# Whole float32 products for the first layer's input projections, and attention's PSUM as three more accumulators

## The chip, the cores and the metric

The kernel runs on one core of one Trainium2 chip. The metric is device time in microseconds (us) of one execution, the median of the runs shown. Five engines take part: TensorE (PE in the profile, with its weight loads as PEld), VectorE (DVE), ScalarE (ACT), GpSimd (POOL) and SyncE (SP), which here only issues the loads of the weights. Each engine works through its own queue in order; semaphores tie the queues together.

## The reference

One step of a two-layer trunk, for 256 prompt positions and 8 sample rows, all float32:

```
for l in range(2):
    h = rmsnorm(x, attn_norm_g[l])
    q, k, v, u = split(h @ w_in[l])        # 2048 -> 1024 + 128 + 128 + 1024
    a = sliding-window attention(rope(q), rope(k), v, sinks)   # 16 heads, window 128
    s = S5 state space over u (64 groups of 16 channels, 64 states each), then z * sigmoid(z @ w_glu + b)
    x = x + concat(rmsnorm(a), rmsnorm(s)) @ w_out[l]
    up = rmsnorm(x) @ w_up[l]              # 2048 -> 2 * 5632
    x = x + (silu(conv(g)) * conv(val)) @ w_down[l]
y = rmsnorm(x)
```

The last rows of k and v, the final states and the last up-projected rows are returned as well.

## The kernel before

The activations are kept transposed: 128 features on the partitions and 264 columns (256 prompt positions and 8 sample rows), so the model width of 2048 is 16 tiles `x[0]` to `x[15]` of 128x264. A *product* gives one tile of 128 output features: it runs over the chunks `k` of the contraction (16 for a projection in, 8 for `oa`, `glu` and `os`), and adds them up in one PSUM accumulator.

**One chunk is three matmuls.** A float32 weight chunk `w` is split as `w = wh + wl`, and the activation as `h = hh + hl`, each part in the type float32r, and `product` issues `wh*hh`, `wh*hl` and `wl*hh`. The weights come from HBM as tiles `raw` of 8 chunks (512 KB, four buffers, loaded in order by SP). `Stream.prep_to` makes from each half of a `raw` tile (a *unit*, 4 chunks, 128x512) the tile `wh`, a cast on ACT (sometimes on DVE), and `wl = raw - wh`, a subtraction on DVE (on POOL for the first four units and where the planner finds DVE late). `Stream.get` is called at each fourth chunk, prepares 4 or 5 units ahead of the one used, and asks for the `raw` tile three ahead. The first layer's activations `h` are split before the layers begin, one ACT and one DVE instruction for each of the 16 tiles; other activations go through `split`.

**Order of the work.** The program is written out by a planner (`Plan`, `Engine.cost`) that keeps a modelled time for each engine. `ORDERS[l]` fixes the order of a layer's products. Between any two chunks `side.tick()` lets the waiting side tasks (generators: attention heads, SSM steps, evictions, norms) issue instructions whose inputs are ready by the modelled times; PE's queue, like the others, is then worked through in that order. `side.until(cond)` ticks, and moves the modelled PE time on, until the condition holds.

**A layer.** `mix_phase` runs 18 projections in (`k`, `v`, `q0` to `q7`, `u0` to `u7`), then 13 or 14 products `oa` (attention's part of the projection out), `glu0` to `glu7`, the rest of `oa`, and `os0` to `os15` (the SSM's part). While the projections run, side tasks rotate q and k, do the eight pairs of attention heads (`heads`), one sample task, and the SSM of each `u` tile in two halves (`ssm_pair`: matmul `xps`, then on DVE `m`, `xr`, four scans, `n`, `G`; then matmul `yps`). The task `ssm_prep` makes the SSM's tables on POOL. A `z` tile (the input of `glu`) needs the SSM of its `u` tile; all eight are needed for each `glu`. Then `ffn_phase` streams the up and down projections, 44 + 44 products of 16 chunks and 48 of 16, 16 and 12.

**Accumulators.** `s_acc` holds two PSUM accumulators for all products. `acc_tile` waits (by modelled time) until one is free; the task that evicts the accumulator gives it back (`take_u`, `take_v`, `take_kq`, `add_half`, `gate_task`, `conv`, `down`). `take_u`, `take_v` and `add_half` need the factor of an RMSNorm (`norm_h.rb`, `norm_a.rb`, `norm_s.rb`) first. Attention has three more PSUM tiles of its own in a mix phase, `s_sps` (two) and `s_ops` (one). The products `os0` and `os1` take their accumulators from `s_sps`; nothing else does after attention.

Of the kernel before, what the change touches and what calls it, by code (L numbers as in the profile page):

```python
# [10 lines left out]
F32 = mybir.dt.float32  # L11
# [28 lines left out]
          "oa11 oa12 glu0 oa13 glu1 glu2 glu3 glu4 glu5 glu6 glu7 oa14 oa15 os0 os1 os2 os3 os4 os5 os6 os7 os8 "  # L40
          "os9 os10 os11 os12 os13 os14 os15").split())
NUNITS = DEPTH * 2720 // UNIT


class Engine:
# [264 lines left out]
def tile_hymba_step(ctx: ExitStack, tc: tile.TileContext, w, xT, consts, gains, small, kc, vc, vc0, ssm_bc, ssm_h0, convp, sconv, kraw, vraw, craw,  # L310
# [14 lines left out]
    s_acc = Slots(nc, ps_acc, "acc", 2, [P, NT])  # L325
    s_ev = Slots(nc, np_, "ev", 2, [P, NT])

    def acc_tile(name):
        side.until(s_acc.there)
        return s_acc.tile(name)  # L330

    bank = Sem(nc, 1)

# [4 lines left out]
    class Stream:  # L338
# [17 lines left out]
        def prep_to(self, n):  # L356
            while self.prep < min(n, NUNITS):
                i = self.prep
                self.load_to(i // 2 + 1)
                src = self.raw[i // 2][:, (i % 2) * UNIT * P:(i % 2 + 1) * UNIT * P]  # L360
                wh = wp.tile([P, UNIT * P], F32R, tag="wh", name=f"wh{i}", bufs=5)
                if i >= 8 and nc.t["dve"] < nc.t["pe"] + -500.0 and nc.t["act"] > nc.t["pe"] + 1000.0:
                    nc.vector.tensor_copy(wh, src)
                else:
                    nc.scalar.copy(wh, src)
                self.wh[i] = (wh, src)
                if i % 2:
                    del self.raw[i // 2]
                self.prep += 1
            while self.low < min(n - (n > 8), NUNITS):  # L370
                i = self.low
                wh, src = self.wh.pop(i)
                wl = wp.tile([P, UNIT * P], F32R, tag="wl", name=f"wl{i}", bufs=4)
                (nc.gpsimd if i < 4 or (nc.t["pool"] < nc.t["pe"] + 0.0 and nc.t["dve"] > nc.t["pe"] + 2000.0) else nc.vector).tensor_tensor(wl, src, wh.bitcast(F32), ALU.subtract)
                self.ready[i] = (wh, wl)
                self.low += 1
# [11 lines left out]
    def product(acc, n, chunk):  # L388

        for k in range(n):  # L390
            if k % UNIT == 0:
                wh, wl = ws.get()
            side.until(lambda: chunk(k) is not None)
            j = (k % UNIT) * P
            hl = chunk(k)
            nc.tensor.matmul(acc, wh[:, j:j + P], hl[:, 0, :], start=(k == 0), stop=False)
            nc.tensor.matmul(acc, wh[:, j:j + P], hl[:, 1, :], start=False, stop=False)
            nc.tensor.matmul(acc, wl[:, j:j + P], hl[:, 0, :], start=False, stop=(k == n - 1))
            side.tick()
# [7 lines left out]

    def set_tiles(s, i, name):
        return setp.tile([P, 2, NT], F32R, tag=f"set{s}_{i}", name=name)


    x = []
# [357 lines left out]
    def mix_phase(l, sets, h, norm_h):  # L770
# [160 lines left out]
        AT = [None] * 8  # L931
        norm_a = Norm(f"a{l}", 1024)
        s_raw, s_rot = Slots(nc, mp, "qraw", 3, [P, NT]), Slots(nc, mp, "qrot", 2, [P, NT])
        s_sps, s_ops = Slots(nc, pm, "sps", 2, [P, 3, P]), Slots(nc, pm, "ops", 1, [P, NPR])
        s_sm, s_mx, s_pT = Slots(nc, mp, "sm", 2, [P, 2, 3 * P]), Slots(nc, mp, "mx", 2, [P, 4, 2, 2]), Slots(nc, mp, "pT", 2, [P, 3, P])

        def rotate(raw, dst, nm):
# [46 lines left out]
        def heads(i, qrot):  # L984
# [47 lines left out]
                    nc.vector.tensor_copy(pT[hh], pps)  # L1032
                    s_sps.give("dve", pps)
            s_sm.give("pe", sm)
            ops = opsd[i] = yield from s_ops.take(f"ops{l}{i}")
            yield "pe", *pT
            for cols, blk, j, first, final in ((slice(0, P), 0, 0, True, True), (slice(P, NPR), 0, 1, True, False),
                                               (slice(P, NPR), 1, 2, False, True)):
# [126 lines left out]
        def take_u(m, acc):  # L1165
            yield from norm_h.wait()
            ude = Y[m]
            rb = norm_h.rb
            yield "dve", acc, rb
            nc.vector.tensor_tensor(ude[:, 0:NPR].rearrange("p (j c) -> p j c", j=2),  # L1170
                                    acc[:, 0:NPR].rearrange("p (c j) -> p j c", j=2),
                                    rb[:, 0:NPR].rearrange("p (c j) -> p j c", j=2), ALU.mult)
            nc.vector.tensor_tensor(ude[:, NPR:], acc[:, NPR:], rb[:, NPR:], ALU.mult)
            s_acc.give("dve", acc)
            side.add(ssm(m, ude), 1)

        def take_v(acc):
            yield from norm_h.wait()
            vsb = yield from s_raw.take(f"vsb{l}")
            yield "dve", acc, norm_h.rb  # L1180
            nc.vector.tensor_tensor(vsb, acc, norm_h.rb, ALU.mult)
            s_acc.give("dve", acc)
            side.add(v_task(vsb))

        def take_kq(nme, acc):
            raw = yield from s_raw.take(f"raw{l}{nme}")
            yield "act", acc
            nc.scalar.copy(raw, acc)
            s_acc.give("act", acc)
            side.add(k_task(raw) if nme == "k" else q_task(int(nme[1]), raw))  # L1190
            if nme == "q7":
                side.add(sample_task(), 0)
# [1 line left out]

        halves = set()

        def add_half(m, acc, norm, nm, own=False, eng="pool"):
            yield from norm.wait()
            t = yield from s_ev.take("ev" + nm)
            yield "dve", acc, norm.rb  # L1200
            nc.vector.tensor_tensor(t, acc, norm.rb, ALU.mult)
            if not own:
                s_acc.give("dve", acc)
            if eng == "pool":
                yield "pool", t
            (nc.gpsimd if eng == "pool" else nc.vector).tensor_tensor(x[m], x[m], t, ALU.add)
            s_ev.give(eng, t)
            halves.add(nm)
# [6 lines left out]
        def gate_task(m, acc):  # L1215
            s2 = yield from s_s2.take(f"s2{l}{m}")
            th = yield from s_ev.take(f"th{l}{m}")
            yield "act", acc
            nc.scalar.activation(th, acc, AF.Tanh, bias=hvec[:, l * 16 + 8 + m:l * 16 + 9 + m], scale=0.5)
            s_acc.give("act", acc)  # L1220
            if m == 7:
                warm()
            yield "dve", th
            nc.vector.scalar_tensor_tensor(s2[:, 0:NPR].rearrange("p (c j) -> p j c", j=2),
                                           th[:, 0:NPR].rearrange("p (j c) -> p j c", j=2), 1.0,
                                           Y[m][:, 0:NPR].rearrange("p (j c) -> p j c", j=2), ALU.add, ALU.mult)
            nc.vector.scalar_tensor_tensor(s2[:, NPR:], th[:, NPR:], 1.0, Y[m][:, NPR:], ALU.add, ALU.mult)
            s_ev.give("dve", th)
            stt = set_tiles(sB, m, f"s{l}{m}")
            yield from split(stt, s2, hgs[:, l * 8 + m:l * 8 + m + 1])  # L1230
            norm_s.add(s2, last=m == 7)
            s_s2.give("act", s2)
            S[m] = stt
            if m == 7:
                norm_s.start()
# [5 lines left out]
        def residual(m, acc):  # L1241
            while f"a{l}{m}" not in halves:
                yield None
            yield from add_half(m, acc, norm_s, f"s{l}{m}", m < 2, "pool" if m < 14 else "dve")
            hl = set_tiles(sC if m < 8 else sA, m % 8, f"h2{l}{m}")
            yield from split(hl, x[m], gain(l, 3, m))
            norm_f.add(x[m])
            h2[m] = hl
            if m == DK - 1:
                norm_f.start()  # L1250
# [2 lines left out]
        lastin = [n for n in ORDERS[l] if n[0] in "uqkv"][-1]  # L1253
        for nme in ORDERS[l]:
            kind, m = nme.rstrip("0123456789"), int(nme.lstrip("uqkvoasgl") or 0)
            if kind == "os" and m < 2:
                side.until(s_sps.there)
                acc = s_sps.tile(f"os{l}{m}", [P, NT])
            else:
                acc = acc_tile((f"in{l}{nme}" if kind in "uqkv" else f"{kind}{l}{m}"))  # L1260
            if kind == "oa":
                product(acc, 8, lambda k: AT[k] if f"A{k}" in done else None)
                side.add(add_half(m, acc, norm_a, f"a{l}{m}"), 0)
# [6 lines left out]
            else:  # L1270
                product(acc, DK, lambda k: h[k])
                side.add(take_u(m, acc) if kind == "u" else take_v(acc) if kind == "v" else take_kq(nme, acc), -2)
                if nme == lastin:
                    done.add("in")
        side.until(lambda: norm_s.rb is not None and "attn" in done)
        mctx.close()
        return h2, norm_f

    def ffn_phase(l, sets, h2, norm_f):
# [20 lines left out]
        def conv(acc, f, rf):  # L1300

            e = s_E.pop()
            nc.vector.tensor_tensor(e[:, 2:], acc, rf, ALU.mult)
            s_acc.give("dve", acc)
            c = s_cv.tile(f"cv{l}{f}")
            return c, conv_gen(c, e, f)

# [61 lines left out]
        def down(m, acc, last):  # L1369
            yield "dve", acc  # L1370
            nc.vector.tensor_tensor(x[m], acc, x[m], ALU.add)
            s_acc.give("dve", acc)
            if last:
                yield "act", x[m]
                norm_n.add(x[m], last=m == DK - 1 and l == DEPTH - 1)
# [49 lines left out]
    for k in range(DK):  # L1425
        if k % UNIT == 1:
            for j in ((0, 1), (2,), (3,), ())[k // UNIT]:
                norm_h.add(x[j], eng=nc.gpsimd)
            ws.prep_to(k // UNIT + 1)
        hl = set_tiles(sets[0] if k < 8 else sets[1], k % 8, f"h{k}")  # L1430
        nc.scalar.activation(hl[:, 0, :], x[k], AF.Copy, scale=gain(0, 0, k))
        some_params(1)
        nc.vector.scalar_tensor_tensor(hl[:, 1, :], x[k], gain(0, 0, k), hl[:, 0, :].bitcast(F32), ALU.mult, ALU.subtract)
        h[k] = hl

    def squares():
        for k in range(4, DK):
# [171 lines left out]
```

## Time and profile before

| | |
|---|---|
| median of 3 runs | 2337.96 us (2332.14 to 2338.8) |
| profiled execution: its time | 2339.3 us |
| profiled execution: its span | 2337.5 us |
| TensorE clock granted, mean over the span | 0.973 of full speed |
| PE busy | 2208.3 us (94%) |
| DVE busy | 1718.0 us (73%) |
| ACT busy | 1272.4 us (54%) |
| POOL busy | 673.7 us (29%) |

All times in the profile count from the start of the span. The busy time of PE includes the pipelined end of each matmul, so it is an upper bound of the time in which the array takes columns. The trace gives most instructions the line of a helper (L116), so they are told apart by the names of their tiles: `in0q<-h,wh` is a matmul of a `q` projection of layer 0, `wl<-raw,wh` the subtraction, `xps`, `m`, `xr`, `n`, `G`, `yps` the steps of the SSM, `sps`, `sm`, `pps`, `ops` those of attention, `eva` and `evs` the evictions of `oa` and `os`.

### The profile page before, as it was taken

To read this page: it belongs to the slowest core of one execution; us is meant where nothing else is said; L and a number is where in the kernel's file an instruction comes from. 1 tells how busy PE (TensorE), PEld (TensorE's weight loads), DVE (VectorE), ACT (ScalarE), POOL (GpSimd) and SP (SyncE) were. 2 spreads that over 40 slices of the span, in tenths; PEclk is the share of its full clock that TensorE was granted. 3 is DMA by queue.
4 is the path that set the end of the run, shared out by engine and by line. 5 is a ranking of instruction groups with operands and counts; after the bars stand their busy time and mean duration, and the time that the engine had idled before them with its cause. 6 is when DMAs were issued, how large, how long until landed. Compare 5 with 4: busy or idle time off the path is not lost.

```text
span 2337.5 us, 47944 instructions
## 1 busy us (share of the span) xinstructions
PE 2208.3 (94%) x18300; PEld 2145.2 (92%) x18300; DVE 1718.0 (73%) x3227; ACT 1272.4 (54%) x2493; POOL 673.7 (29%) x895
## 2 busy tenths in 40 slices
PE   7988799999999999999998878999999999999997
PEld 6866688999999999999997767989999999999997
DVE  8898987877657776577778979777775677756764
ACT  5655455555445554455555564655554455545554
POOL 6565636711001110011236555341110011101112
PEclk9999899999999999999999989999999999999998
DMA  6322344555655555555553313545555555555553
GB/s 201 128 74 81 102 139 163 174 181 181 198 181 179 180 192 185 180 179 191 190 166 105 106 65 117 170 163 179 180 180 182 179 181 181 181 181 181 180 188 128
DMA packets 107447, 378.24 MB, mean 162 GB/s; under 512 B 14386, under 2 KB 16706, under 8 KB 107168
## 3 DMA queue, kind: packets, MB, share of 16 engines
q1 hardware_dynamic: 101664, 361.10, 46.3%
q0 software_dynamic: 3248, 13.48, 1.9%
q8 instruction: 144, 2.36, 0.4%
q10 hardware_dynamic: 2304, 0.59, 0.1%
q14 instruction: 87, 0.71, 0.1%
HBM read 371.18 MB, written 6.73 MB: 162 GB/s over the span
## 4 chain that ended last, share of the span: by engine, by line
PE 73%; DVE 6%; POOL 2%; issue 1%; ACT 0%; DMA 0%; DVEq 0%; ACTq 0%; POOLq 0%
PE d L116 22%; PE g L116 21%; PE v L116 21%; PE oa L116 2%; PE in1q L116 1%; DVE wl L116 1%; DVE xr L116 1%; PE glu L116 1%; PE os L116 1%; PE in1u L116 1%; DVE m L116 1%; DVE G L116 1%; POOL ssq_f L116 1%; POOL x L116 0%; DVE sm L116 0%
## 5 line engine op out<-in xcount | busy, mean ns | idle before, releaser
L116 DVE TENSOR_TENSOR wl<-raw,wh 128x512 fp32r<-128x512 f32 x1323 | 978.3, 743 | 368.7 <-PE d L116 171.1
L116 ACT CAST wh<-raw 128x512 fp32r<-128x512 f32 x1358 | 836.3, 620 | 712.8 <-PE d L116 236.8
L116 PE MATMUL g<-h,wh 128*128 128x264 f32 x2816 | 524.2, 286 | 1.7 <-DVE E L116 1.1
L116 PE MATMUL v<-h,wh 128*128 128x264 f32 x2816 | 521.7, 285 | 0.0
L116 PE MATMUL d<-ff,wh 128*128 128x264 f32 x2816 | 516.0, 284 | 0.0
L116 PEld LDWEIGHTS g<-h,wh 128*128 128x128 f32 x2816 | 441.1, 190 | 2.5 <-DVE E L116 1.5
L116 PEld LDWEIGHTS v<-h,wh 128*128 128x128 f32 x2816 | 439.2, 189 | 0.2
L116 PEld LDWEIGHTS d<-ff,wh 128*128 128x128 f32 x2816 | 436.9, 188 | 0.0
L116 POOL COPY cout<-E 128x10 f32<-128x10 f32 x176 | 100.6, 572 | 1148.1 <-DVE E L116 1148.1
L116 PE MATMUL g<-h,wl 128*128 128x264 f32 x1408 | 404.3, 287 | 0.0
L116 PE MATMUL v<-h,wl 128*128 128x264 f32 x1408 | 402.8, 286 | 0.0
L116 PE MATMUL d<-ff,wl 128*128 128x264 f32 x1408 | 400.5, 284 | 0.0
L116 PEld LDWEIGHTS g<-h,wl 128*128 128x128 f32 x1408 | 266.9, 190 | 0.0
L116 PEld LDWEIGHTS v<-h,wl 128*128 128x128 f32 x1408 | 265.5, 189 | 0.0
L116 PEld LDWEIGHTS d<-ff,wl 128*128 128x128 f32 x1408 | 265.1, 188 | 0.0
L116 DVE SCALAR_TENSOR_TENSOR cv<-E,cw,cv 128x256 f32<-128x256 f32 x352 | 174.4, 496 | 21.5 <-ACT cv L116 2.4
L116 PE MATMUL oa<-a,wh 128*128 128x264 f32 x512 | 109.4, 311 | 28.6 <-DVE eva L116 18.4
L116 PEld LDWEIGHTS oa<-a,wh 128*128 128x128 f32 x512 | 88.0, 208 | 33.7 <-issue 20.3
L116 ACT ACTIVATE cv<-E,cw 128x264 f32<-128x264 f32 x176 | 106.9, 609 | 2.3 <-DVE E L116 2.3
L116 PE MATMUL os<-s,wh 128*128 128x264 f32 x512 | 95.7, 286 | 3.7 <-DVE evs L116 3.5
L116 PEld LDWEIGHTS os<-s,wh 128*128 128x128 f32 x512 | 79.4, 188 | 6.4 <-issue 4.2
L116 DVE TENSOR_TENSOR E<-g,rb_f 128x264 f32<-128x264 f32 x88 | 38.0, 432 | 59.2 <-PE g L116 59.2
(316 smaller groups left out, 3026.7 us busy)
## 6 DMA issues: line engine op xcount, KB each, us to landing
raw<-in_w_dram SPq DMA_DIRECT2D x680, 512.0 KB, 3.3
bc<-in_ssm_bc_dram POOLq DMA_DIRECT2D x16, 256.0 KB, 3.2
x<-in_xT_dram SPq DMA_DIRECT2D x16, 132.0 KB, 3.9
out_dram<-hn SPq DMA_DIRECT2D x8, 264.0 KB, 2.6
sc<-in_sconv_dram POOLq DMA_DIRECT2D x2, 704.0 KB, 5.5
kct<-in_kc_dram POOLq DMA_DIRECT2D x2, 512.0 KB, 7.5
vct<-in_vc_dram POOLq DMA_DIRECT2D x2, 508.0 KB, 9.4
out_dram<-in_kraw_dram POOLq DMA_DIRECT2D x1, 1016.0 KB, 7.7
```

What stands on the lines that cost most here:

```text
L116: return real(*args, **kw)
```

## The change

Four things in the code, in both layers unless said otherwise:

- Units of the first layer's 18 projections in are *plain* (`plain(i)` is true for the first 72 of the 680 units of layer 0). `prep_to` makes neither `wh` nor `wl` for them; the `raw` tile itself goes to `product`, which issues one matmul per chunk, of float32 weights and float32 activations.
- The first layer's `h` tiles are float32 and written whole by one instruction each, by ACT for even `k` and by DVE (`tensor_scalar`) for odd `k`. The second instruction of each is gone.
- `acc_tile` takes a list of further slots. Once a mix phase's attention is done, its products may also take `s_sps` and `s_ops` (whose tile grows from 256 to 264 columns); `os13` to `os15` may not. `acc_give` returns an accumulator to the slots that it is from. `os0` and `os1` have no place of their own any more.
- At the end of `mix_phase` the planner waits until all three are free again.

```
+PLAIN = 18 * DK // UNIT
+PLAINS = (0,)
+def plain(i):
+    return i // (NUNITS // DEPTH) in PLAINS and i % (NUNITS // DEPTH) < PLAIN
...
-    def acc_tile(name):
-        side.until(s_acc.there)
-        return s_acc.tile(name)
+    owner = {}
+    def acc_tile(name, more=()):
+        of = [s_acc, *more]
+        side.until(lambda: any(s.there() for s in of))
+        s = next(s for s in of if s.there())
+        t = s.tile(name, [P, NT])
+        owner[t.tensor.name] = s
+        return t
+    def acc_give(eng, t):
+        owner.pop(t.tensor.name).give(eng, t)
...
+                if plain(i):                      # Stream.prep_to, first loop
+                    self.ready[i] = (src, None)
+                    if i % 2:
+                        del self.raw[i // 2]
+                    self.prep += 1
+                    continue
...
+                if plain(i):                      # Stream.prep_to, second loop
+                    self.low += 1
+                    continue
...
+            if wl is None:                        # product
+                nc.tensor.matmul(acc, wh[:, j:j + P], hl, start=(k == 0), stop=(k == n - 1))
+                side.tick()
+                continue
...
+    def whole_tile(s, i, name):
+        return setp.tile([P, 2, NT], F32, tag=f"set{s}_{i}", name=name)[:, 0, :]
...
-            if kind == "os" and m < 2:
-                side.until(s_sps.there)
-                acc = s_sps.tile(f"os{l}{m}", [P, NT])
-            else:
-                acc = acc_tile((f"in{l}{nme}" if kind in "uqkv" else f"{kind}{l}{m}"))
+            lent = (s_sps, s_ops) if "attn" in done and not (kind == "os" and m > 12) else ()
+            acc = acc_tile((f"in{l}{nme}" if kind in "uqkv" else f"{kind}{l}{m}"), lent)
...
-        side.until(lambda: norm_s.rb is not None and "attn" in done)
+        side.until(lambda: norm_s.rb is not None and "attn" in done and len(s_sps.free) == 2 and len(s_ops.free) == 1)
...
-        hl = set_tiles(sets[0] if k < 8 else sets[1], k % 8, f"h{k}")
-        nc.scalar.activation(hl[:, 0, :], x[k], AF.Copy, scale=gain(0, 0, k))
+        hk = whole_tile(sets[0] if k < 8 else sets[1], k % 8, f"h{k}")
+        if k % 2:
+            nc.vector.tensor_scalar(hk, x[k], gain(0, 0, k), None, ALU.mult)
+        else:
+            nc.scalar.activation(hk, x[k], AF.Copy, scale=gain(0, 0, k))
         some_params(1)
-        nc.vector.scalar_tensor_tensor(hl[:, 1, :], x[k], gain(0, 0, k), hl[:, 0, :].bitcast(F32), ALU.mult, ALU.subtract)
-        h[k] = hl
+        h[k] = hk
```

## Rows read from the trace of the kernel before

**Rows 1.** The page's busy tenths in 40 equal slices of the span.
```profile
PE   7988799999999999999998878999999999999997
DVE  8898987877657776577778979777775677756764
```
**Rows 2.** Windows: length, busy us (x instructions) by engine, PE clock, DMA share, GB/s.
```profile
51.00:223.00 172.00, 150.22 (x1354) 129.99 (x1353) 149.68 (x333) 103.19 (x274) 103.52 (x118) 0.92 0.31 99
224.00:308.00 84.00, 62.59 (x568) 55.64 (x569) 79.49 (x137) 39.87 (x82) 50.32 (x49) 0.90 0.30 97
308.00:394.00 86.00, 83.19 (x678) 80.20 (x677) 67.24 (x120) 51.34 (x108) 38.39 (x37) 0.98 0.47 160
1182.00:1388.00 206.00, 175.93 (x1589) 154.74 (x1587) 172.81 (x383) 111.22 (x291) 110.03 (x124) 0.94 0.34 108
1388.00:1456.00 68.00, 56.99 (x511) 52.51 (x512) 62.37 (x118) 35.02 (x78) 36.21 (x34) 0.86 0.33 106
```
**Rows 3.** Timeline of PE where stages begin or end: start us, us, instructions.
```profile
51.26 0.81 PE L116 MATMUL in0v<-h,wh 128*128 128x264 f32 x2
...
222.60 0.28 PE L116 MATMUL in0u<-h,wl 128*128 128x264 f32 x1
224.43 0.48 PE L116 MATMUL oa<-a,wh 128*128 128x264 f32 x2 [1.55 <-DVE nm_a L116]
...
307.68 0.48 PE L116 MATMUL glu<-z,wh 128*128 128x264 f32 x2 [4.12 <-DVE eva L116]
```
**Rows 4.** Groups by tile, 51:219, and ACT's 0:219; xcount, busy us, mean ns, idle before.
```profile
L116 DVE TENSOR_TENSOR wl<-raw,wh 128x512 fp32r<-128x512 f32 x48 | 44.4, 938 | 8.4 <-ACT wh L116 4.6 <-PE in0q L116 2.7 <-PE in0v L116 1.0
...
L116 ACT CAST wh<-raw 128x512 fp32r<-128x512 f32 x74 | 44.4, 615 | 25.9 <-PE in0q L116 8.6 <-PE in0u L116 8.5 <-PE in0k L116 3.8
```
**Rows 5.** The chain of waits in the FFN: start us, us, what.
```profile
501.82 5.84 PE g L116 x48
```
**Rows 6.** Timeline of PE and its weight loads around a whole float32 matmul (nps_s).
```profile
343.58 0.41 PE L116 MATMUL os<-s,wh 128*128 128x264 f32 x2
343.83 0.28 PE L116 MATMUL os<-s,wl 128*128 128x264 f32 x1
343.95 0.61 PE L116 MATMUL nps_s<-nd_s,cs 128*128 128x264 f32 x2
344.20 0.60 PE L116 MATMUL os<-s,wh 128*128 128x264 f32 x2
344.64 0.28 PE L116 MATMUL os<-s,wl 128*128 128x264 f32 x1
...
343.83 0.31 PEld L116 LDWEIGHTS nps_s<-nd_s,cs 128*128 128x128 f32 x2
```
**Rows 7.** Timelines of ACT, POOL and PE at the start of the kernel.
```profile
21.86 0.62 ACT L116 CAST wh<-raw 128x512 fp32r<-128x512 f32 x1 [1.97 <-PE in0k L116]
...
24.24 13.12 POOL L116 TENSOR_TENSOR ssq_in<-ssq_in,spare 128x264 f32<-128x264 f32 x12 [5.31 <-ACT spare L116]
...
48.58 1.00 PE L116 MATMUL nps_in<-nd_in,cs 128*128 128x264 f32 x2 [3.58 <-DVE nd_in L116]
```
**Rows 8.** DMA issues (page): out<-in queue op xcount, KB each, median us to landing.
```profile
raw<-in_w_dram SPq DMA_DIRECT2D x680, 512.0 KB, 3.3
```
**Rows 9.** Groups by tile, PE: first 224:308, then 1388:1456.
```profile
L116 PE MATMUL xps<-U,bt 64*128 64x136 f32 x48 | 4.4, 300 | 1.3 <-DVE G L116 1.3
...
L116 PE MATMUL xps<-U,bt 64*128 64x136 f32 x32 | 2.9, 301 | 0.0
```
**Rows 10.** Who waited for whom, PE, 51:308: us in total, times, longest.
```profile
PE oa L116 <- DVE eva L116: 10.8, 4, 6.6
```
**Rows 11.** Timeline of POOL late in os of layer 0.
```profile
379.14 1.19 POOL L116 TENSOR_TENSOR x<-x,evs 128x264 f32<-128x264 f32 x1
381.34 1.29 POOL L116 TENSOR_TENSOR ssq_f<-ssq_f,sq_f 128x264 f32<-128x264 f32 x1 [1.01 <-ACT sq_f L116]
382.59 1.19 POOL L116 TENSOR_TENSOR x<-x,evs 128x264 f32<-128x264 f32 x1
```
**Rows 12.** Groups of the whole span (page).
```profile
L116 DVE TENSOR_TENSOR wl<-raw,wh 128x512 fp32r<-128x512 f32 x1323 | 978.3, 743 | 368.7 <-PE d L116 171.1
```

More of the change, by code (lines that the diff above doesn't have):

```diff
@@ L933, in mix_phase @@
         s_raw, s_rot = Slots(nc, mp, "qraw", 3, [P, NT]), Slots(nc, mp, "qrot", 2, [P, NT])
-        s_sps, s_ops = Slots(nc, pm, "sps", 2, [P, 3, P]), Slots(nc, pm, "ops", 1, [P, NPR])
+        s_sps, s_ops = Slots(nc, pm, "sps", 2, [P, 3, P]), Slots(nc, pm, "ops", 1, [P, NT])
         s_sm, s_mx, s_pT = Slots(nc, mp, "sm", 2, [P, 2, 3 * P]), Slots(nc, mp, "mx", 2, [P, 4, 2, 2]), Slots(nc, mp, "pT", 2, [P, 3, P])
@@ L1034, in heads @@
             s_sm.give("pe", sm)
-            ops = opsd[i] = yield from s_ops.take(f"ops{l}{i}")
+            ops = opsd[i] = (yield from s_ops.take(f"ops{l}{i}"))[:, 0:NPR]
             yield "pe", *pT
@@ L1173, in take_u @@
             nc.vector.tensor_tensor(ude[:, NPR:], acc[:, NPR:], rb[:, NPR:], ALU.mult)
-            s_acc.give("dve", acc)
+            acc_give("dve", acc)
             side.add(ssm(m, ude), 1)
@@ L1181, in take_v @@
             nc.vector.tensor_tensor(vsb, acc, norm_h.rb, ALU.mult)
-            s_acc.give("dve", acc)
+            acc_give("dve", acc)
             side.add(v_task(vsb))
@@ L1188, in take_kq @@
             nc.scalar.copy(raw, acc)
-            s_acc.give("act", acc)
+            acc_give("act", acc)
             side.add(k_task(raw) if nme == "k" else q_task(int(nme[1]), raw))
@@ L1195, in mix_phase, with add_half @@
         halves = set()
-        def add_half(m, acc, norm, nm, own=False, eng="pool"):
+        def add_half(m, acc, norm, nm, eng="pool"):
             yield from norm.wait()
@@ L1201, in add_half @@
             nc.vector.tensor_tensor(t, acc, norm.rb, ALU.mult)
-            if not own:
-                s_acc.give("dve", acc)
+            acc_give("dve", acc)
             if eng == "pool":
@@ L1219, in gate_task @@
             nc.scalar.activation(th, acc, AF.Tanh, bias=hvec[:, l * 16 + 8 + m:l * 16 + 9 + m], scale=0.5)
-            s_acc.give("act", acc)
+            acc_give("act", acc)
             if m == 7:
@@ L1243, in residual @@
                 yield None
-            yield from add_half(m, acc, norm_s, f"s{l}{m}", m < 2, "pool" if m < 14 else "dve")
+            yield from add_half(m, acc, norm_s, f"s{l}{m}", "pool" if m < 14 else "dve")
             hl = set_tiles(sC if m < 8 else sA, m % 8, f"h2{l}{m}")
@@ L1303, in conv @@
             nc.vector.tensor_tensor(e[:, 2:], acc, rf, ALU.mult)
-            s_acc.give("dve", acc)
+            acc_give("dve", acc)
             c = s_cv.tile(f"cv{l}{f}")
@@ L1371, in down @@
             nc.vector.tensor_tensor(x[m], acc, x[m], ALU.add)
-            s_acc.give("dve", acc)
+            acc_give("dve", acc)
             if last:
```

## The prediction, made before the changed kernel was run

> **What bounds the kernel now.** I read the slices first. PE is at 9 almost everywhere and falls to 7 or 8 in slices 1 to 6 and 23 to 26, the two mix phases; there, and only there, DVE is at 7 to 9 [rows 1]. The FFN between them is a closed chain of matmuls: 48 of a 16-chunk product in 5.84 us, 0.122 us for each [rows 5]. The change leaves it alone, so the question lies in layer 0 before the FFN, and, for the lent accumulators, in the same place of layer 1.
>
> Then the windows, one for each stage, with the timeline of PE to find their ends [rows 2, 3]. The reader is to see three stages in layer 0. (a) 0 to 51.26 us: the products k, q0, u0, u1, then a wait of PE for the norm of the input. (b) 51.26 to 222.9 us: the other 14 projections, with attention and part of the SSM beside them; PE 150 of 172 us busy, DVE 150. (c) 224.4 to 307.7 us: 14 products oa and the rest of the SSM, up to the first glu; DVE 79.5 of 84 us busy, PE 62.6. From there PE is full again (83.2 of 86). So in (c) DVE is the bound, and in (b) neither engine is full: PE waits for results that DVE, with a full queue, gives late. Last the groups by tile: of DVE's work in (b) 48 subtractions wl take 44.4 us, 938 ns each [rows 4].
>
> **What a chunk costs.** Now it is three float32r matmuls, 3 x 0.122 = 0.365 us. A whole float32 matmul of the same shape stands in the trace: nps_s, two records. Between the os pairs at 343.95 and the wl at 344.64 lie 0.69 us; a pair and its wl are 0.25 us apart without it (343.58 to 343.83), so it costs 0.44 us [rows 6]. That is 0.08 us more than the three; times 16 chunks 1.25 us for each product, 7.1 instead of 5.84. In 18 products PE gets 288 x 0.08 = 23 us of work more at full clock. DVE loses the subtractions of 72 units, less those that POOL does, 48 of them in (b), and ACT 72 casts (of the 74 counted, two belong to oa), 72 x 0.615 = 44 us [rows 4].
>
> The Trainium skill ("FP8 and Floating Point Precision", TensorE Precision Notes) says that true float32 takes four passes of the array. Four at the spacing above would be 0.49 us, another 13 us of PE work over the 288 chunks, and at worst a time of 2316. The row says 0.44, in two records of 0.22, and the measurement decides.
>
> **Stage (a): 7 us less.** PE waits at 48.58 for the factor of the norm, which starts from the sum of squares on POOL; POOL began the 12 sums of that at 24.24, after 5.31 us of idling for ACT's squares, and ACT's queue held casts that waited for PE (the one at 21.86) [rows 7]. Without the casts the squares can follow the last h, some 6 us earlier, and the 13.1 us of sums end near 31 instead of 37.4; DVE's part behind them has fewer subtractions in front. So the factor should be there near 40 to 43. PE needs for k 16 x 0.89 = 14 us, an estimate: twice 0.445, since it starts at the lower clock; from about 7 us that is 21, and with three products of 7.1 it is 43. v then starts at 44 and not at 51.26. Bounds: nothing (the factor stays late: DVE's chain of setup is in front of it) to 9 us (PE alone).
>
> The raw tiles are now held until PE has used them. SP's load of the tile three ahead waits for PE to end the one before: 24 chunks, 24 x 0.44 = 10.6 us ahead of its use, and a load lands in 3.3 us [rows 8]. SP has nothing else queued behind it but further loads. I cost it at nothing; without that cover it would be up to 3.3 us for each of 36 tiles, 119 us.
>
> **Stage (b): 9 us less.** PE gets 14 x 1.25 = 17.5 us more, DVE 44 us less. PE's busy time of 150.2, which is itself an upper bound, becomes 168 if all of the addition shows in it, still under the stage's 171.6; what PE now spends waiting (21 us of idling, and low clock: 0.92) shrinks with DVE's queue. The attention heads and the SSM steps need DVE for 150 - 44 = 106 us of a stage of about 162, so they no longer come late. Bounds: 17.5 longer (nothing of it is hidden, no wait shrinks) to 13 shorter (PE without a wait, at the 0.98 clock of the stretch after 308 [rows 2]: 150 x 0.92/0.98 = 141, and 17.5 more, 158). I take 162, near that end, because with a third less on DVE PE is the engine with the least slack.
>
> **Stage (c): 16 us less.** The backlog of the SSM that DVE brings into (c) is six halves (48 records of xps, 8 to a half). Layer 1 enters its own with four (32 records) and takes 1388 to 1455.5, that is 67 us with 13 oa, against 83 here [rows 2, 9]. In (b) DVE has 44 us less to do, and uses about 9 of that for the shorter stage; with some 7 us of DVE work for each half the backlog falls to the four that wait for the last two u tiles whatever happens. So (c) becomes 67. Bounds: nothing, to 27 less, which leaves 56: 14 products of 2.92 and 15 us for the other matmuls (an estimate from the windows' 62.6 us busy).
>
> **The lent accumulators: 3 us less.** PE stands 10.8 us in (c) for an eviction eva [rows 10]. With five accumulators it would not, but where DVE is the bound (c) ends with DVE; for layer 0 that is in the 67 already. Layer 1's (c) is 92% DVE, with 5.6 us not busy [rows 2]: 3 us, bounds 0 to 6. Against it stands that an oa issued earlier puts its two subtractions ahead of an SSM step: two for each of three products, 6 x 0.9 = 5.4 us, repaid later in the same stage. In os nothing: from the tenth product on POOL repeats x, wait for ACT's square, ssq_f every 3.45 us (379.14 to 382.59) [rows 11], while PE would need 2.92. That loop feeds the next stage, and more accumulators don't shorten it; bounds 0 to 4 us for each layer. The wait for free slots at the end of the phase is the planner's and stops no engine.
>
> **Sum.** 7 + 9 + 16 + 3 = 35 us off the profiled execution's 2339.3 (span 2337.5) is 2304. It lies 1.3 us above the median of the runs, so 2303.
>
> **Rivals.**
> - *PE takes the bound over in (b).* The 17.5 us show in full: PE runs its queue of 168 us and idles nearly as now when attention's chain is late. (b) is some 10 us longer, (a) and (c) as forecast, the lent slots 2 less: 7 - 10 + 16 + 2 = 15 us, 2323. For it: both engines at 87% in (b) are coupled, and layer 1 needs 206 us for 18 products with DVE at 84% [rows 2]. Against: the waits are on the side of DVE.
> - *DVE sets it all.* From 51.26 to 307.7 DVE is busy 229 us, 89%. Without 44 us of it, at the same share, 208 us; from 44 that is 252 us, not 307.7: 56 us less, 2282. For it: subtractions take 938 ns in (b) and 743 over the whole span [rows 4, 12], so DVE and POOL get in each other's way, and less of one speeds up the other. The Trainium skill ("SBUF — State Buffer", SBUF: two separate sides) says that a DVE instruction with two SBUF inputs and a GpSimd instruction lock each other out; the two means fit, and by it POOL gains too. Against: PE's 168 us in (b) leave no room for all of it.
> - *Slower: the weights of whole float32 don't hide.* The row that gives 0.44 is a single matmul between others. Each has two weight loads (0.31 us for the two, overlapped, at 343.83) [rows 6]. In a chain of 16 the next pair might not be loaded under the matmul before: 0.75 us for each chunk, 16 x 0.31 = 5 us for each product, 70 us in (b) and 15 in (a), less the 32 above that come from DVE: 2338 + 53 = 2391. It decides from about 0.57 us a chunk on, where 288 x 0.12 eats the 35. Against: the following os pair in that row starts without a gap.
> - *The change does nothing that counts.* The factor of the norm stays at 50, (b) grows by 17.5 and (c) gives the same back: 2338.
>
> **Chances.** Forecast 0.62, PE bound 0.17, DVE sets it all 0.10, no difference 0.05, slower 0.06. The forecast's own range by its terms is 2290 to 2316. For eight in ten the range reaches over both neighbours: 2278 to 2328. A measurement of this kernel tells 0.3%, 7 us, from no change: faster 0.88, same 0.05, slower 0.07 (a hundredth of it from the far end of the case without a difference).
>
> **What would show it.** In the trace of the changed kernel: in0q with two records to a chunk, 0.22 apart, and 7.1 us to an undisturbed product (0.75 a chunk proves the slower rival). v starts near 44 (a). The last in0u ends near 206, the first glu starts near 275, and the xps of stage (c) count 32 (b, c). DVE's busy share in (b) falls to about two thirds; if it stays near 87%, DVE's work is not what I take it for. The stretch from the first glu to the first g, and the FFN, keep their lengths to 2 us. I would be wrong if PE's idling in (b) stays with DVE no longer full: then the waits are latencies of the side tasks' chains and not a queue, and only (a) and (c) give anything.

## The result

The changed kernel takes 2310.78 us (median of 4 runs, 2309.78 to 2314.54) against 2338.38 us before; the ratio is 0.989, 95% interval 0.988 to 0.991: 27.6 us, or 1.1%, faster. 2303 was forecast, with a range of 2278 to 2328. The profiled execution is the slowest of the four, 2314.54 us with a span of 2312.8; the two spans differ by 24.7 us.

The page of the kernel after, busy tenths in 40 slices; it answers to [rows 1]:

```profile
PE   8999899999999999999998888999999999999997
DVE  6667977777557775677778979777775677656764
```

DVE's first four slices fall from 8, 8, 9, 8 to 6, 6, 6, 7, and four of PE's first five rise by one. DVE's slices 21 to 27, layer 1's mix phase, are as they were. The stage ends, from PE's timelines (us):

| | first v | last in0u | first oa | first glu | first g | FFN of layer 0 | layer 1's mix | rest |
|---|---|---|---|---|---|---|---|---|
| before | 51.3 | 222.6 | 224.4 | 307.7 | 394.0 | 787.5 | 358.8 | 797.3 |
| after | 50.0 | 223.6 | 225.3 | 287.1 | 368.8 | 786.6 | 360.8 | 796.6 |

The last three columns are lengths. All of the gain lies between the last in0u and the first g: 171.4 us become 145.2. The 18 projections, the only products that were changed, end 1.0 us *later*. The rest moves by -0.9, +2.0 and -0.7.

PE's timeline after (start us, us, instructions), the places of [rows 3] and the start:

```profile
33.14 1.25 PE L122 MATMUL nps_in<-nd_in,cs 128*128 128x264 f32 x2 [3.02 <-DVE nd_in L122]
37.71 1.08 PE L122 MATMUL rpsk<-raw0k,cs 128*128 128x264 f32 x2
...
44.52 5.61 PE L122 MATMUL in0u<-h,raw 128*128 128x264 f32 x24
49.96 1.28 PE L122 MATMUL in0v<-h,raw 128*128 128x264 f32 x5
...
222.07 2.13 PE L122 MATMUL in0u<-h,raw 128*128 128x264 f32 x4
...
225.34 0.81 PE L122 MATMUL oa<-a,wh 128*128 128x264 f32 x2
...
287.09 0.40 PE L122 MATMUL glu<-z,wh 128*128 128x264 f32 x2
```

Each chunk is two records, and 24 records fill 44.52 to 49.96: 0.227 us each. The matmul of the norm, at 48.58 in [rows 7], is at 33.14, and the wait of 4.12 us before glu [rows 3] is gone.

The windows after: length, busy us (x instructions) of PE, PEld, DVE, ACT, POOL, then PE's granted clock, DMA share, GB/s. The first three answer to [rows 2]; the last one is from PE's start to the end of the projections:

```profile
51.00:223.00 172.00, 159.70 (x1192) 119.72 (x1191) 118.69 (x323) 76.64 (x230) 86.75 (x108) 0.97 0.31 98
223.00:287.00 64.00, 56.94 (x511) 51.27 (x511) 57.72 (x100) 30.77 (x64) 32.32 (x32) 0.92 0.40 132
287.00:369.00 82.00, 79.86 (x642) 78.34 (x641) 64.24 (x115) 50.83 (x106) 37.22 (x35) 1.00 0.50 165
...
7.00:223.00 216.00, 199.14 (x1363) 150.91 (x1364) 146.77 (x409) 93.20 (x266) 120.96 (x162) 0.96 0.37 119
```

The same last window of the kernel before:

```profile
7.00:223.00 216.00, 183.88 (x1555) 160.35 (x1555) 191.22 (x429) 128.57 (x329) 134.59 (x155) 0.92 0.36 118
```

This pair is the centre of the result. In the same 216 us PE is busy 15.3 us longer and idles 15.3 us less (32.1 to 16.9), while DVE has 44.5 us less to do. PE's new work took the place of time in which PE had waited, and its granted clock rose from 0.92 to 0.96; nothing was left over for an earlier end. DVE's 44.5 us come back only later, as a smaller remainder of the SSM.

### The profile page after: what moved, and what is told of

It reads as the page before. It is cut to its first block, busy times and chain, and to the rows that moved or that the text cites. A ratio compares the mean times of both kernels' runs of the same rounds, so it can differ in the third digit from the quotient of the medians.

```text
span 2312.8 us, 47095 instructions
## 1 busy us (share of the span) xinstructions
PE 2212.7 (96%) x18012; PEld 2126.3 (92%) x18012; DVE 1651.3 (71%) x3162; ACT 1226.9 (53%) x2408; POOL 640.4 (28%) x884
## 5 line engine op out<-in xcount | busy, mean ns | idle before, releaser
L122 DVE TENSOR_TENSOR wl<-raw,wh 128x512 fp32r<-128x512 f32 x1262 | 921.3, 733 | 360.7 <-PE d L122 170.3
L122 ACT CAST wh<-raw 128x512 fp32r<-128x512 f32 x1286 | 792.5, 620 | 683.6 <-PE d L122 236.8
L122 PE MATMUL oa<-a,wh 128*128 128x264 f32 x512 | 103.0, 299 | 5.7 <-ACT a L122 4.9
L122 PE MATMUL oa<-a,wl 128*128 128x264 f32 x256 | 76.5, 299 | 13.6 <-DVE wl L122 13.6
```

The costliest lines, as they stand in the source:

```text
L122: return real(*args, **kw)
```

## The experiments

Two theories stood at the start. *Relief*: the gain is DVE's freed time, and whole products cost PE something. *Lending*: the extra accumulators free PE in the stage of the oa products. A third is that the norm's early factor carries the gain. All stage ends and the busy time from the start to the first glu (windows of that length), with the medians:

| | first v | last in0u | first glu | first g | PE busy | DVE busy | median | ratio, 95% |
|---|---|---|---|---|---|---|---|---|
| before | 51.3 | 222.6 | 307.7 | 394.0 | 246 | 274 | 2338 | |
| after | 50.0 | 223.6 | 287.1 | 368.8 | 256 | 207 | 2310.8 | 0.988 to 0.991 |
| e1 | 50.6 | 222.6 | 289.4 | 369.9 | 254 | 208 | 2311.8 | 0.988 to 0.991 |
| e2 | 51.2 | 220.5 | 295.7 | 393.1 | 241 | 264 | 2334.4 | 0.998 to 1.000 |
| e3 | 40.2 | 203.0 | 271.5 | 353.2 | 233 | 213 | 2295.7 | 0.981 to 0.984 |
| e4 | 52.4 | 234.3 | 306.4 | 388.2 | 263 | 258 | 2329.9 | 0.997 to 0.999 |
| e5 | 50.6 | 223.8 | 287.4 | 369.2 | 256 | 206 | 2311.4 | 0.987 to 0.992 |
| e6 | 51.6 | 236.3 | 299.9 | 381.6 | 257 | 241 | 2321.3 | 0.990 to 0.995 |
| e7 | 55.7 | 222.5 | 291.4 | 373.2 | 245 | 261 | 2313.4 | 0.988 to 0.991 |
| e8 | 51.7 | 223.2 | 295.3 | 377.1 | 253 | 243 | 2317.8 | 0.989 to 0.994 |
| e9 | 49.9 | 223.6 | 295.3 | 377.0 | 251 | 241 | 2327.1 | 0.995 to 0.998 |
| e10 | 58.6 | 245.1 | 305.7 | 387.4 | 253 | 250 | 2329.1 | 0.996 to 0.998 |
| e11 | 43.4 | 223.4 | 286.9 | 368.6 | 254 | 203 | 2311.7 | 0.988 to 0.991 |
| e12 | 49.8 | 222.7 | 286.2 | 368.1 | 254 | 204 | 2310.2 | 0.988 to 0.992 |

The kernel before ran beside each group, at medians of 2335.9 (e1 to e4), 2336.9 (e5 to e7), 2336.8 (e8 to e10) and 2336.7 (e11, e12); ratios are to these.

### e1: whole products without lending

```
-        of = [s_acc, *more]
+        of = list(more) or [s_acc]
-            lent = (s_sps, s_ops) if "attn" in done and not (kind == "os" and m > 12) else ()
+            lent = (s_sps,) if kind == "os" and m < 2 else ()
```

> Whole float32 products in layer 0, accumulators as before the change (os0 and os1 from the score tiles, nothing else lent). Theory (the gain is the relief of VectorE in layer 0): 2311 + 4 = 2315 us, the first glu of layer 0 within 5 us of 287, layer 1 as before. Rival (the lent accumulators carry the gain, because TensorE no longer stands for evictions in oa): 2325 us or more, with TensorE again waiting some 15 us for eva between the first oa and the first glu.

Measured: 2311.76 us, within 1 us of the change. The whole products alone give the whole gain. PE still stands for evictions between the first oa and the first glu, about as long as in the kernel before (10.8 us [rows 10]), so these waits were not what held the time:

```profile
PE oa L122 <- DVE eva L122: 10.2, 2, 7.8
```

### e2: lending without whole products

```
-PLAINS = (0,)
+PLAINS = ()
```

and the float32r pairs of `h` as before.

> Three matmuls for every chunk as before the change, but attention's PSUM lent. Theory: 2338 - 3 = 2335 us; the waits for eva go, the first glu comes no more than 3 us earlier because VectorE's queue ends there. Rival (lending carries the gain): 2322 us or less, the first glu near 292.

Measured: 2334.44 us; the interval holds no change and up to 0.2% of gain. The trace shows where the lent slots' time goes. PE's timeline of e2 at the first glu:

```profile
295.70 0.40 PE L122 MATMUL glu<-z,wh 128*128 128x264 f32 x2
...
299.48 0.39 PE L122 MATMUL glu<-z,wh 128*128 128x264 f32 x1 [1.32 <-DVE z L122]
...
307.13 1.07 PE L122 MATMUL yps<-G,cp 128*32 128x128 f32 x14 [4.89 <-DVE G L122]
...
311.35 1.06 PE L122 MATMUL glu<-z,wh 128*128 128x264 f32 x2 [1.51 <-ACT z L122]
```

With more accumulators PE reaches glu at 295.70 and not at 307.7, and is held up inside it, from 299.71 to 311.35, for z tiles whose SSM steps (G, yps) are not done; the four waits shown are 9.6 us together. The first g comes at 393.1 against 394.0: the wait is moved, not removed. The theory had allowed glu only 3 us; there it came nearly as early as the rival said (292), and the time did not follow. In this kernel lending is worth next to nothing while DVE is behind.

### e3: the subtraction left out, three matmuls kept

```
+                    wh, src = self.wh.pop(i)
+                    self.ready[i] = (wh, wh)      # plain units, instead of the subtraction
```

The third matmul reads `wh` in place of `wl`, so `wh*hh` is added twice and the low part of the weights is missing: the result is not the reference's, and the kernel serves for its time alone. The instructions of PE are as many as before the change; `h` is split as before and ACT's casts stay.

> Leaves out the subtraction in layer 0's projections in: three float32r matmuls for a chunk with the rounded weights in the third too, ScalarE's casts and the split activations kept. VectorE is relieved as in the change, and TensorE has not the 23 us more. Theory (TensorE is the new bound of the projections): the stretch from v to the last u falls from 174 to about 157 us and the time to 2311 - 15 = 2296 us. Rival (the waits there are the latencies of the attention and SSM chains): the stretch stays at 170 or more, the time within 5 us of 2311.

Measured: 2295.74 us, 40 us under the kernel before: DVE's relief without PE's extra work. Its window from PE's start to the end of the projections (columns as above; the change's is 7:223):

```profile
7.00:203.00 196.00, 177.40 (x1632) 156.55 (x1633) 149.06 (x422) 125.47 (x330) 114.91 (x153) 0.96 0.41 134
```

DVE's busy time up to the last in0u is about that of the change (149.06 and 146.77). PE's is 177.40 and not 199.14, and the projections end 20.6 us earlier. So in the changed kernel it is PE's work, not DVE's, that sets the end of the projections. Of the 21.7 us that it has more, 20.6 show there and 15.6 at the first g. The time is the theory's. The stretch from v to the last in0u is 162.8 us, between the 157 of the theory and the 170 of its rival; 9.8 of the 20.6 us are there already when v starts (40.2 and not 50.0).

### e4: whole products, the subtraction still done

```
+                    src = self.ready[i][0]        # plain units
+                    wl = wp.tile([P, UNIT * P], F32R, tag="wl", name=f"wl{i}", bufs=4)
+                    (nc.gpsimd if ... else nc.vector).tensor_tensor(wl, src, src, ALU.subtract)
```

Nothing reads this `wl`; it only keeps DVE and POOL occupied.

> The change, with the 72 subtractions of layer 0's projections issued as before, into tiles that nothing reads; the casts stay away. VectorE's relief is taken back, the larger products stay. Theory: the time goes to 2338 us or above (about 2340: 25 us back from VectorE's queue, with 23 us more of TensorE work beside it, less a few for the earlier norm). Rival (the gain comes from ScalarE, whose casts are gone, and from the earlier norm): 2318 us or less.

Measured: 2329.93 us, between the two expectations, 6 us under the kernel before and 19 above the change. Its windows:

```profile
51.00:234.00 183.00, 167.72 (x1211) 123.89 (x1210) 149.47 (x366) 77.22 (x226) 102.56 (x117) 0.95 0.29 94
234.00:306.00 72.00, 58.47 (x529) 51.87 (x529) 65.03 (x111) 36.53 (x74) 39.31 (x39) 0.93 0.36 117
```

With the subtractions back, DVE is busy 50 us longer up to the first glu, which moves by 19.3 us to 306.4. So some 19 of the 27 us need these subtractions gone. An early start is not enough by itself: attention's first scores (sps) come at 63.7 us here and at 63.9 in the change, against 76.4 in the kernel before. The 6 us that e4 itself gains belong to the rest of the change (no casts on ACT, one instruction for each `h`, lending), less the price of PE's work; they were not taken apart further.

### e5: whole products in both layers

```
-PLAINS = (0,)
+PLAINS = (0, 1)
```

and layer 1's `hn` tiles written whole, as `h` is.

> Layer 1's projections in are whole float32 products as well (its input tiles written whole by one instruction each at the end of layer 0's FFN). Theory (relief of VectorE pays in the backlog stage, the larger products cost most of their 16 to 23 us once TensorE is the bound of the projections): in layer 1 there is no late input norm to win back and less backlog, so the two nearly cancel: mix phase of layer 1 between 350 and 358 us against 358 to 361, the time 2305, range 2300 to 2312. Rival (the gain is of the start of layer 0 alone): layer 1 only pays TensorE's price, mix phase 370 us or more, 2322.

Measured: 2311.41 us, no measurable difference from the change, at the slow end of the theory's range. Layer 1's mix phase takes 356.5 us (360.8 in the change), which lies in the range named for it. Layer 1's 18 projections, the change and then e5:

```profile
1155.40:1358.50 203.10, 178.88 (x1588) 157.72 (x1587) 169.17 (x373) 110.84 (x287) 103.61 (x117) 0.92 0.34 110
```

```profile
1153.20:1368.90 215.70, 196.02 (x1335) 149.34 (x1333) 134.87 (x360) 78.48 (x234) 88.02 (x116) 0.96 0.32 103
```

The projections take 12.6 us longer, and the stage behind them, to the first glu, is 12.7 us shorter (53.6 us, not 66.3). What is left is 4 us between the two: the first oa follows the last u after 2.5 us and not 6.8. In layer 0 PE's idle time up to the end of the projections fell by 15.3 us and hid the price; here it falls from 24.2 to 19.7 us. 11.0 us of what is left are waits for ACT's copy of q (rpsq for raw1q); why they arise was not settled.

### e6, e7, e10: whole products for some of the projections

```
+PLAIN_SET = frozenset([0, 1, 2, 10, 11, 12, 13, 14, 15, 16, 17])     # e6
+PLAIN_SET = frozenset([0, 1, 2, 3, 4])                               # e7
+PLAIN_SET = frozenset([10, 11, 12, 13, 14, 15, 16, 17])              # e10
-    return i // (NUNITS // DEPTH) in PLAINS and i % (NUNITS // DEPTH) < PLAIN
+    return i < PLAIN and i * UNIT // DK in PLAIN_SET
```

`h` is in its split form, and the whole products read its high part alone; the low parts are made by a side task on DVE (16 instructions, 11.0 us). So these kernels carry work that the change doesn't.

> Products 3 to 9 of layer 0 (u1, v, q1, q2, q3, u2, q4) go back to three float32r matmuls, the other eleven stay whole. The whole ones read the rounded activations (their low part is left out there), because the chip's SBUF has no room for both forms. VectorE is about 60% busy in that stretch and TensorE full, so theory: TensorE gets 7 x 1.25 = 9 us less, VectorE 28 subtractions (20 us) more in its slack, the time falls by 4 to 8 us to about 2305. Rival (VectorE's relief counts everywhere, its slack is only waiting inside chains): 2311 + 8 = 2319 or more.

> Only products 0 to 4 of layer 0 (k, q0, u0, u1, v) are whole, with rounded activations (low part left out there), the other thirteen three matmuls. It keeps the early norm and little else. Theory: the norm and the first rotation come 10 us earlier as in the change, and VectorE, which sets the rest again, carries that through: 2338 - 9 = 2329 us. Rival (an earlier start only makes a longer wait further on): 2336 or more.

> The converse: only products 10 to 17 of layer 0 (q5, q6, u3, q7, u4 to u7) whole, with rounded activations, the first ten three matmuls. Theory: no gain, TensorE's price of 10 us shows and 32 subtractions buy little: 2338 to 2346 us, the last in0u after 226. Rival (VectorE's total counts): 32 subtractions or 24 us less at 0.6, 14 us, against a hidden price: 2326 us or less.

Measured: 2321.28, 2313.39 and 2329.11 us. Five whole products at the start (with lending) give nearly all of the gain; the last eight alone give 0.2 to 0.4%. For e6 the theory fell (work put into DVE's idle time in the middle cost time, though part of this is the low parts of `h`), for e7 both expectations were too slow, and e10 lies between its two, nearer the rival. The windows up to the last in0u, e7 and then e10:

```profile
51.00:222.00 171.00, 152.29 (x1407) 131.18 (x1406) 156.49 (x366) 98.97 (x270) 99.08 (x110) 0.94 0.34 107
```

```profile
51.00:245.00 194.00, 173.12 (x1392) 137.54 (x1391) 151.18 (x358) 103.42 (x278) 109.40 (x130) 0.92 0.29 94
```

In e7 DVE is still at 92% of that stage and PE at 89%, and the projections end where they did before, with less left over after them. Up to the first glu DVE has 13 us less to do than in the kernel before (261 and 274), and the glu comes 16 us earlier at the same share (90 and 89%). In e10 the window holds 13.4 us more of PE's work than the change's 172 us, v starts 8.6 us later, and the end comes at 245.1. Why e6 and e10 end their projections later than both the kernel before and the change stays open.

### e8, e9: the first ten, in one layer or in both

```
+PLAIN_N = (10, 0)      # e8
+PLAIN_N = (10, 10)     # e9
```

with `h` as in e6; the low parts follow the norm.

> Products 0 to 9 of layer 0 whole (with rounded activations, low part left out there), the last eight three matmuls; the low parts of the activations are made after the input norm. Theory from the runs so far (a larger product late in the stage delays the last u tiles by its full 1.25 us, while the subtractions it saves there buy little; in the first ten the saved subtractions buy more than the price): faster than the change, 2311 - 8 + 3 for the low parts = 2306 us, the last in0u before 218. Rival (what counts is VectorE's total up to the first glu): 32 subtractions more for VectorE, 24 us at the share of 0.6 that the middle seven showed: 2311 + 14 - 10 for TensorE = 2315 or more.

> The same in both layers: products 0 to 9 of each layer whole with rounded activations. Theory: in layer 1 the first ten alone give the mix phase 8 us less than before the change, 351 against 359, 2298 us in all. Rival (VectorE's total counts): layer 1 keeps 356 or more, 2311 or more.

Measured: 2317.8 and 2327.1 us. More whole products than five bring nothing more (the intervals of e7 and e8 overlap, so that ten are worse than five is not shown), and ten in layer 1 cost 9 us. Both missed the theory's number and went as the rival had it. Why ten in layer 1 cost and all 18 (e5) don't stays open.

### e11: the norm's task later

```
+        while ws.use < 9:
+            yield None
```

at the head of the task that sums the squares of the input.

> The change, but the squares for the input norm are held back until the third product begins, as they came by themselves before the change. VectorE stays relieved, only the norm's factor, the rotations and the first SSM step come some 6 to 9 us later (first rotation near 46 instead of 38). Theory (VectorE's relief carries most of the gain, an earlier norm no more than its own head start): 2311 + 3 to 9, 2317 us. Rival (over all kernels so far the time of the first glu follows the moment of the first rotation, up to 2.7 us for each us; the early norm is the cause): 2311 + 20, 2331 us or more.

Measured: 2311.73 us, as the change, less than even the theory's 3 to 9 us and 20 from the rival. PE's timeline of e11:

```profile
42.82 0.71 PE L122 MATMUL rpsk<-raw0k,cs 128*128 128x264 f32 x2 [0.47 <-ACT rb_in L122]
43.37 1.14 PE L122 MATMUL in0v<-h,raw 128*128 128x264 f32 x4
...
222.60 1.40 PE L122 MATMUL in0u<-h,raw 128*128 128x264 f32 x4
```

The factor is used at 42.82 and not at 37.71, v starts at 43.37 and not at 49.96, and the last in0u is where it was. POOL's first rotation, of k, is back where the kernel before has it; POOL before, in the change and in e11:

```profile
51.38 0.74 POOL L116 TENSOR_TENSOR raw0k<-raw0k,rope 128x264 f32<-128x264 f32 x1 [1.26 <-PE rpsk L116]
```

```profile
39.11 0.75 POOL L122 TENSOR_TENSOR raw0k<-raw0k,rope 128x264 f32<-128x264 f32 x1
```

```profile
51.00 0.75 POOL L122 TENSOR_TENSOR raw0k<-raw0k,rope 128x264 f32<-128x264 f32 x1
```

POOL makes the SSM's tables first in this order, so it is a swap and not a pure delay, and attention's first sps still comes early (62.7 us). It does show that neither 5 us of the norm nor 6.6 us of v's start reach the end of the projections.

### e12: the other half of `h` on DVE

```
-        if k % 2:
+        if k % 2 == 0:
```

> The change with the two engines that write the first layer's h tiles swapped (VectorE the even ones, ScalarE the odd ones): the same work, another order from the planner. It measures what a mere reordering does. Theory: 2311 within 4 us, so differences of 8 us and more between the kernels above are of their work. Rival (the planner's order scatters the time by 10 us whatever the work): more than 8 us off.

Measured: 2310.21 us, 0.6 us from the change: a mere reordering of the start moves nothing that can be told. None of the versions that compute the reference beats the change measurably.

## Why the prediction held, and where it failed

**The total.** Sign and range held, the total partly by luck: one stage gained 17 us less than its term and the stages behind it 10 us more, and the two errors cancel in part. The forecast said 35 us off the profiled execution in the terms -16 (stages (a) and (b), to the last in0u), -16 (stage (c)) and -3 (lending). Measured, by the spans: +1.0 for the projections, -21.5 for (c) from the first oa to the first glu (83.3 to 61.8 us), -4.6 from there to the first g (86.3 to 81.7), and +0.4 for all the rest. Two readings of the slices were loose, without weight in the sum: layer 1's dip of PE is in slices 22 to 25, and DVE is at 7 or 8 in many slices of the FFN as well [rows 1].

**The chunk.** Right: two records of 0.22 us, weight loads hidden under them, as the row of nps_s had it [rows 6]; the rival of weights that don't hide is out. For PE's added work 23 us were forecast. An estimate from the busy time of the in0 matmuls from 7 to 224 times the granted clock (150.8 x 0.96 less 136.1 x 0.92) gives 19.5 us; by the spacing of the chain, 0.453 against 0.365 us a chunk, it is 25. The Trainium skill ("FP8 and Floating Point Precision", TensorE Precision Notes) gives four passes for true float32. Four at 0.122 us would be 0.49, an estimate from that count, and the trace has 24 records, 12 chunks, in 5.44 us, 0.45 each. By the skill's count the chunk would be about a tenth too dear.

**Stage (a).** The mechanism was right: without casts before them ACT's squares start at 15.23 and POOL's sums at 15.79, where [rows 7] had 24.24. ACT and POOL after:

```profile
15.23 3.54 ACT L122 ACTIVATE spare<-x 128x264 f32<-128x264 f32 x11
```

```profile
15.79 9.78 POOL L122 TENSOR_TENSOR ssq_in<-ssq_in,spare 128x264 f32<-128x264 f32 x12 [2.95 <-ACT spare L122]
```

The factor was there even before the 40 to 43 of the forecast. The product k took 9.7 us (7.08 to 16.79) and not the 14 of the forecast. That v starts at 49.96 and not at 44 all the same is because PE ran rpsk, rpsq, bt_ps, k_ps and xps among the chunks of u0 and u1, work that came after v before. But the seven microseconds were counted as a gain of the whole, and e11 shows that a start of v 6.6 us apart leaves no trace at the last in0u.

**Stage (b): the step that failed** is "what PE now spends waiting (21 us of idling, and low clock: 0.92) shrinks with DVE's queue ... I take 162". It took 173.6. DVE's share fell to 69% (118.69 of 172), "about two thirds" as said, and the clock rose to 0.97. But PE's idling fell only from 21.8 to 12.3 us, and with 159.70 us of its own work PE is the engine that sets the stage (e3). The added 17.5 us show as 9.5 us of busy time, at the higher clock. PE's waits for DVE's sm and DVE's for PE's sps, before and after (PE from 51 to 223, DVE from 50 to 224; us in total, times, longest):

```profile
PE pps L116 <- DVE sm L116: 4.4, 6, 1.6
...
DVE sm L116 <- PE sps L116: 1.9, 2, 1.3
```

```profile
PE pps L122 <- DVE sm L122: 4.7, 4, 3.2
PE k_ps L122 <- ACT bt L122: 3.9, 1, 3.9
```

```profile
DVE sm L122 <- PE sps L122: 12.3, 7, 2.7
DVE mx L122 <- ACT mx L122: 8.9, 5, 2.3
```

DVE now stands much longer for PE's sps, and PE still as long as before for DVE's sm, a step later in the same head, although DVE idles for 31% of the stage. This reads as the latency of attention's chain and not a queue; the prediction had named this as what would make it wrong. Another 3.9 us are one wait for the SSM's tables (bt). The rival "PE takes the bound over in (b)" had the mechanism, and too high a price: the stage grew by 2.3 us and not by 10, since PE's idling did shrink by nearly half.

**Stage (c)** gave more than forecast. The backlog is what was said, four halves. The group after, PE from 224 to 287 (xcount | busy us, mean ns | idle before), answers to [rows 9]:

```profile
L122 PE MATMUL xps<-U,bt 64*128 64x136 f32 x32 | 3.5, 344 | 0.0
```

48 became 32, and the stage 61.8 us, 5 less than layer 1's 67 that served as its measure, and this with 14 oa products where layer 1 has 13. Without lending (e1) it is 65.4, so lending explains most of this difference; but e1's first g is only 1.1 us later, so what lending gains there is mostly given back. What the forecast left out is the stretch after the first glu, 4.6 us shorter and not the same within 2: all of it is in the glu products, which take 23.1 us and not 27.7 from the first to the last. Before, the wait of 4.12 us for eva [rows 3] stands ahead of the first glu, and glu then starts at a granted clock of 0.60, holds the yps of the last half of the SSM (40 records, 310.76 to 312.72) and a wait of 0.58 us for z. After, nothing of this is there, and the clock is 1.00 from 287.10 on. PE before:

```profile
307.70:310.50 2.80, 2.80 (x15) 2.80 (x15) 2.70 (x5) 0.57 (x3) 1.79 (x2) 0.60 0.53 187
...
310.76 1.07 PE L116 MATMUL yps<-G,cp 128*32 128x128 f32 x16
...
314.30 0.85 PE L116 MATMUL glu<-z,wh 128*128 128x264 f32 x2 [0.58 <-ACT z L116]
```

That is the backlog and not the accumulators: e1 has 80.5 us there without lending, and e2 with lending alone 97.4.

**Lending.** Forecast 3 us; measured nothing that can be told (e2's interval allows up to 0.2%). In layer 1 the wait of 7.5 us for an eviction did go; before and after, PE from 1330 to 1470:

```profile
PE oa L116 <- DVE eva L116: 7.5, 1, 7.5
```

```profile
PE oa L122 <- DVE wl L122: 7.3, 4, 3.0
PE xps L122 <- DVE G L122: 6.0, 2, 3.8
```

7.3 us for subtractions stand in its place (and 6.0 for G, where 4.7 stood), and layer 1's mix phase takes 360.8 us, not 358.8. The forecast had written this repayment down ("puts its two subtractions ahead of an SSM step") and still kept a gain; the bound of zero was the right end.

**"DVE sets it all"** fell short because it left PE out. Up to the first glu the kernel before has DVE at 89% and PE at 80%; after, PE at 89% and DVE at 72%. In the other kernels the busier of the two is at 83 to 90%. The two effects don't add up by engine: DVE's relief is worth 40 us while PE's products are cheap (e3), and 19 while they are dear (e4 against the change); PE's extra work costs 15 us once DVE is free, and next to nothing while DVE is the one that is late: e4, with PE's extra work and the subtractions, has its first g 4.9 us *before* that of e2, which lends as it does and keeps the three matmuls. This last comparison is not pure, since e4 also lacks ACT's casts and the second instruction for each `h`.

## What to carry to other kernels

When work is moved from one engine to another in a stage where both are busy for 80 to 90% of the time, compare the busy sums of both up to the stage's end; here the gain ended where the second engine became the longer one. A forecast that freed waits will raise that engine's share needs a reason for every wait that is to go. Follow the freed time to where it is repaid: here it did nothing at the end of the stage that was changed, and everything in the one behind it. More accumulators only moved a wait here, while the engine that feeds the next product was itself late.

## What the runs showed that was not expected

- A change of the start by 5 to 10 us (the norm's factor, v's start) can vanish altogether in a stage in which PE is busy 90 to 93% of the time: e11 and the change end the projections at 223.4 and 223.6.
- Instructions that the change doesn't touch became shorter in the mean: in the first 270 us the SSM's scans on DVE take 478 ns each (634 before) and POOL's `n` 1440 ns (1571), while the subtractions that remain take 895 ns as before (896). The means, by group and tile, of the kernel after:

```profile
L122 DVE TENSOR_TENSOR_SCAN xr<-mag,xr 128x128 f32<-128x128 f32 x64 | 27.6, 478 | 0.0
L122 POOL TENSOR_TENSOR n<-xr,tab 128x512 f32<-128x512 f32 x16 | 23.0, 1440 | 25.5 <-DVE xr L122 25.5
```

  With the subtractions put back (e4) the scans take 510 ns and `n` 1549, so only part of it hangs on them. The shortest scan takes 390 ns in both kernels and the median 418 and 400, so for the scans it is mostly that fewer are held up for long; for `n` the median falls too, from 1642 to 1284. What holds them up is not shown.
